# Hybrid DeltaNet and RWKV decoder block on one core: modulation weights bound to steps of the matmul stream, pinned joins, earlier transposes and another prologue

## The chip, the cores and the metric

The kernel runs on one core of one Trainium2 chip. The metric is the device time of one execution in microseconds (us); lower is better. The five engines are named as in the profile: PE (TensorE, matrix products), DVE (VectorE), ACT (ScalarE), POOL (GpSimd) and SP (SyncE, which here only issues DMAs). Each engine works through its own list of instructions in order.

## The reference

One decoder block over 512 tokens of width 1024, in float32. A conditioning vector gives six modulation vectors of 1024; two mixers run beside each other and are merged by gates; a gated feed-forward block with a short convolution follows.

```python
cond = jax.nn.silu(c)
mod = cond @ w_ada[i] + b_ada[i]
shift1, scale1, gate1, shift2, scale2, gate2 = jnp.split(mod[:, None, :], 6, axis=-1)
h = rms_norm(x, norm1_w[i]) * (1.0 + scale1) + shift1
p = h @ w_in[i]
qkv_a, z_a, b_a, a_a, p_b, gl_a, gl_b = split_cols(p, IN_SIZES)
y_a = gated_deltanet(...)      # chunks of 64 tokens, a triangular solve in each
y_b = rwkv7_time_mix(...)      # likewise, computed in chunks by the kernel
merged = sigmoid(gl_a) * (y_a @ w_branch_gdn[i]) + sigmoid(gl_b) * (y_b @ w_branch_rwkv[i])
x = x + gate1 * (merged @ w_out[i])
h = rms_norm(x, norm2_w[i]) * (1.0 + scale2) + shift2
x = x + gate2 * conv_glu(h, w_ffn_in[i], conv_ffn[i], w_ffn_out[i])
return rms_norm(x, norm_f_w)
```

## The kernel before

Activations lie with the features on the 128 partitions and the 512 tokens along the row. A product tile is 128 output features by 512 tokens in one PSUM bank, summed over blocks of 128 input features. Each block takes three matmuls (`mm3`): weights and activations are split into a high part in a shorter format and the float32 remainder, and high·high, high·low and low·high are added. A weight tile arrives as `raw` by DMA, ACT casts it to `whi`, DVE subtracts to `wlo` (`split`).

**The stages**, with their times in the profiled execution: a prologue with the sum of squares of x and the first norm (to 20 us); seven product tiles in which each hidden block is used as soon as it is normed (`first_tiles`, to 61); then the rest of the input projection, as filling between the parts of the two mixers. Each mixer inverts its chunk matrices (`solve`): 32x32 diagonal blocks on DVE and POOL, then the joins, 256 matmuls of 32x32 in two parts with ACT copies between them (L594 and L604, near 205 for the first mixer and 388 for the second), then a recurrence over eight chunks. The products of the first branch (`bg`) start at 335; gate tiles, second branch (`br`), output projection (`o`, residual at L1027) follow, then the second norm (563), the feed-forward products (`fi`, `fo`) and the final norm.

**What sets the order.** Products wait in a list, `queue`. `fill(n)` in the mixers' code draws n groups of three matmuls from it, `need(labels)` draws until given tiles are done, `stream` makes them. A scheduler then moves the emitted instructions by their dependencies and its own model of time; a dependency with the reason "place" binds the order without a semaphore. So what each engine's list looks like is known only after the build.

**The modulation weights.** 48 columns of 128 values, each a dot product of a row of `w_ada` (1024 long, per partition) with the condition. The first 16 (shift and scale of the first norm) are read during the first tiles by `ada`. The other 32 columns are read in halves of 512 (`ada_half`, L208 the DMA, L209 the DVE reduce with its accumulator read), 64 halves in all, with one tile `wada` of one buffer. `product(..., late=n)` asks for n halves when its tile begins; what is left is emitted ahead of `A2`, the scale of the second norm, which needs columns 32 to 39 of `mod`. `mod` 24 to 31 are its shifts; 16 to 23 gate the first residual; 40 to 47 gate the last.

**The second norm.** The residual of the last output tile comes in two halves of 256 tokens (`halves`), so that the norm of the first half (L307 to L309) can begin while PE works on the second.

**Transposes.** `to_natural` turns 128x128 blocks on PE (L616) and copies quarters out of PSUM (L619), for the second mixer after the `bg` products, into another buffer.

Of the kernel before, what the change touches and what calls it, by code (L numbers as in the profile page):

```python
# [23 lines left out]
T = 512  # L24
# [31 lines left out]
def body(ctx, tc, io, out, tap=lambda name, ap: None):  # L56
# [53 lines left out]
    one = const.tile([128, 128], F32, name="one")  # L110
    for k in range(KT):
        sp.dma_start(xT(k), io["xT"][k])
        if k == 3:
            sp.dma_start(cond, io["c"])
    sp.dma_start(cols, io["cols"])
# [12 lines left out]
    kc = const.tile([128, 4], F32, name="kc")  # L128
    for j, v in enumerate((EPS, LNX)):
        pool.memset(kc[:, j:j + 1], v)  # L130
    pool.memset(one, 1.0)
# [46 lines left out]
    last = {"step": None, "hold": False, "gate": None, "norm": None}  # L178
# [4 lines left out]
    def mm3(p, w, j, x, start, stop):  # L183
        hi, lo = (a[j] for a in w)
        xh, xl = x
        i = pe.matmul(p, hi, xh, start=start, stop=False)  # L186
        if last["hold"]:
            tc.add_manual_dep(i.ins, last["step"].ins.name, after, reason="place")
        pe.matmul(p, hi, xl, start=False, stop=False)  # L189
        pe.matmul(p, lo, xh, start=False, stop=stop)  # L190
        return i
# [13 lines left out]
    def ada_half(j, u):  # L205
        w = wp.tile([128, T], F32, name="wada", tag="wada")
        part = slice(T * u, T * u + T)
        sp.dma_start(w, io["w_ada"][j][:, part])  # L208
        i = dve.tensor_tensor_reduce(out=w, in0=w, in1=cond[:, part], scale=1.0,  # L209
                                 scalar=half[:, j:j + 1] if u else col("b_ada", j), op0=ALU.mult, op1=ALU.add,  # L210
                                 accum_out=(mod if u else half)[:, j:j + 1])
        if last["gate"] is not None:
            tc.add_manual_dep(i.ins, last["gate"].ins.name, after, reason="place")
            last["gate"] = None

    first_half = []
# [13 lines left out]
    def stream():  # L230
        while queue:
# [113 lines left out]

    table(SILU)
    fn(cond, cond, AF.Silu)
    table(EXP)
    total = tmp("rs")
    for k in range(KT):  # L350
        sq = total if k == 0 else tmp("sq")
        act.activation(sq, xT(k), AF.Square)
# [3 lines left out]
    pe.matmul(p, one, total, start=True, stop=True)  # L356
# [4 lines left out]
    first_ps = [mm(), mm(), pa(), pa(), pc(), pc(), pc()]  # L361
# [4 lines left out]
    first_w = []  # L366

    def load_ada(k):
        for j in ((0,), (1, 2))[k] if k < 2 else (k + 1,):
            if j < KT:  # L370
                w = slot((2, 3, 8, 9, 12)[j]) if j < 5 else slot2((0, 2, 1)[j - 5])
                first_w.append(w)
                sp.dma_start(w[:, 0:D], io["w_ada"][8 + j])
                sp.dma_start(w[:, D:2 * D], io["w_ada"][j])

    def first_h(k):
# [3 lines left out]
        act.activation(A1[:, k:k + 1], mod[:, 8 + k:9 + k], AF.Identity, scale=col("norm1", k), bias=col("norm1", k))  # L380
# [5 lines left out]
    def inproj(t, evac, psum=mm, begin=None):  # L386
        queue.append(product(t, io["w_in"][t], hx, evac, psum, late=4 if t >= T_GB else 3 if t >= T_GA else 0, begin=begin))
# [99 lines left out]
    last["gate"] = dve.scalar_tensor_tensor(gl, s3, -1.0, bc(nea), op0=ALU.mult, op1=ALU.mult)  # L487
# [65 lines left out]
    def solve(sv, name, work):  # L553
# [9 lines left out]
        sp.dma_start(lt, lsc)  # L563
# [22 lines left out]
        yield  # L586
        for h in range(2):
# [3 lines left out]
            for i in range(16):  # L591
                for e in range(2):
                    lo_r, hi_r = slice(64 * e, 64 * e + 32), slice(64 * e + 32, 64 * e + 64)
                    pe.matmul(p[hi_r, i, :], sv[lo_r, 16 * h + i, 32:64], t1[lo_r, 16 * h + i, :],  # L594
                              start=True, stop=True)
            fill(2)
            for e in range(2):
# [3 lines left out]
            for i in range(16):  # L601
                for e in range(2):
                    lo_r, hi_r = slice(64 * e, 64 * e + 32), slice(64 * e + 32, 64 * e + 64)
                    pe.matmul(p[lo_r, i, :], ht[hi_r, i, :], sv[hi_r, 16 * h + i, 32:64],  # L604
                              start=True, stop=True)
            fill(2)
            for e in range(2):
                lo_r = slice(64 * e, 64 * e + 32)
                act.mul(sv[lo_r, i_, 32:64], p[lo_r], -1.0)

# [98 lines left out]
    for b in range(4):  # L709
# [3 lines left out]
        fill(1)  # L713
    for _ in gsolve:
        pass
# [153 lines left out]
    for ct in range(4):  # L869
        zt, sg = tmp("sg"), tmp("rs")  # L870
        sp.dma_start(zt, zsc[ct])
# [6 lines left out]
    insert([product(("bg", n), io["w_bg"][n], gx, spill(ysc[n])) for n in range(KT)])  # L878
    need(("bg", KT - 1))
# [5 lines left out]
    kb = [ct4(slot(2)), bh]  # L885
    to_natural(bh, lambda e, c: kb[e][hs(e), :, c * C:(c + 1) * C], True)
    to_natural(kh, lambda e, c: kb[e][hs(1 - e), :, c * C:(c + 1) * C], True)
# [124 lines left out]
    for n in range(KT):  # L1012
        if n in (0, 3):
            g = KT - 2 + n // 3
            queue.append(product(T_GB + g, io["w_in"][T_GB + g], hx, last_gate(g), ahead=1))
        queue.append(product(("br", n), io["w_br"][n], bx, merge(n), begin=merge_in(n), ahead=1))
# [88 lines left out]
    for i in range(7, 2 * NF):  # L1105
        queue.append(product(("fi", i), io["w_fi"][i], h2, (glu_up if i % 2 else glu_gate)(i // 2)))
# [38 lines left out]
def _arrays(inputs):  # L1145
# [35 lines left out]
    for e in range(2):  # L1181
# [12 lines left out]
        "c": np.broadcast_to(f["c"], (128, D)),  # L1194
# [29 lines left out]
```

## Time and profile before

| | us |
|---|---|
| median of 3 runs (lowest to highest) | 935.42 (933.39 to 936.28) |
| the profiled execution's own time | 937.31 |
| its span | 935.6 |
| PE busy | 876.3 |
| DVE busy | 533.3 |
| ACT busy | 419.2 |
| mean granted clock of PE | 0.983 |

The span runs from the first to the last instruction; 1.7 us lie around it. A PE that is busy at half the granted clock counts as busy, so a share of 94% is not the share of the full rate. Idle time of PE is told by the instruction that ended it.

### The profile page before, as it was taken

Reading aid. Unit: us, or ns where it says so; the run is one execution under the profiler, and the core shown is the slowest. Engines: PE = TensorE matmul, PEld = TensorE weight load, DVE = VectorE, ACT = ScalarE, POOL = GpSimd, SP = SyncE. Lnnn points to the kernel's source line nnn. Section 1 sums busy time; section 2 is a strip of 40 time slices with the busy share of each in tenths; the row PEclk is TensorE's granted clock in tenths of the full one; section 3 lists DMA queues with packets and bytes.
Section 4 is the critical chain, followed back from the end, with each engine's and each line's share of the span. In section 5 each row is a group of like instructions: output and inputs, shape, how many; then the busy total and the mean of one; then the engine's idle time right before and its main releaser. Section 6 shows DMA issues by size and latency. Waiting matters only on the chain.

```text
span 935.6 us, 13853 instructions
## 1 busy us (share of the span) xinstructions
PE 876.3 (94%) x5459; PEld 687.7 (74%) x5459; DVE 533.3 (57%) x858; ACT 419.2 (45%) x680; POOL 95.2 (10%) x91
## 2 busy tenths in 40 slices
PE   2999999999989978899999999999999999999996
PEld 1886577677656666677668888888888888888885
DVE  5987859824696786255476537564445445332233
ACT  5367543734554747632465335343333333333231
POOL 1000300000352300001230120000000000010112
PEclk9999999997999989899999999999999999999998
DMA  9841245363323367644546542322322322533322
GB/s 332 283 149 67 91 105 185 109 166 112 103 82 113 69 213 267 162 147 148 183 158 202 171 141 84 111 91 92 109 92 90 105 99 90 179 98 100 107 80 91
DMA packets 81119, 125.72 MB, mean 134 GB/s; under 512 B 26045, under 2 KB 42813, under 8 KB 80990
## 3 DMA queue, kind: packets, MB, share of 16 engines
q1 hardware_dynamic: 81054, 124.83, 42.2%
q8 instruction: 43, 0.70, 0.3%
q14 instruction: 22, 0.18, 0.1%
HBM read 110.13 MB, written 14.16 MB: 133 GB/s over the span
## 4 chain that ended last, share of the span: by engine, by line
PE 69%; DVE 10%; DMA 6%; ACT 6%; issue 6%; POOL 2%; SPq 0%; DVEq 0%; POOLq 0%; ACTq 0%
PE ps_mm L186 19%; PE ps_mm L189 18%; PE ps_mm L190 18%; DMA wada<-in_w_ada 4%; DVE wlo L148 2%; PE ps_pc L181 2%; DVE wada L209 1%; ACT tmp_rs L94 1%; PE ps_pc L186 1%; PE ps_pc L189 1%; PE ps_pc L190 1%; ACT slot L619 1%; PE ps_pa L186 1%; PE ps_pa L189 1%; PE ps_pa L190 1%
## 5 line engine op out<-in xcount | busy, mean ns | idle before, releaser
L186 PE MATMUL ps_mm<-hh,whi 128*128 128x512 f32 (+1 forms) x642 | 264.2, 412 | 9.8 <-ACT hh L308 3.4
L148 DVE TENSOR_TENSOR wlo<-raw,whi 128x1024 fp32r<-128x1024 f32 (+2 forms) x140 | 161.2, 1152 | 176.2 <-ACT whi L145 170.6
L190 PE MATMUL ps_mm<-hh,wlo 128*128 128x512 f32 (+1 forms) x642 | 255.0, 399 | 1.3 <-DVE wlo L148 1.3
L189 PE MATMUL ps_mm<-hl,whi 128*128 128x512 f32 (+1 forms) x642 | 253.8, 396 | 0.0
L145 ACT CAST whi<-raw 128x1024 fp32r<-128x1024 f32 (+2 forms) x140 | 137.1, 979 | 259.7 <-PE ps_mm L189 198.4
L186 PEld LDWEIGHTS ps_mm<-hh,whi 128*128 128x128 f32 x642 | 121.5, 190 | 46.8 <-issue 8.5
L190 PEld LDWEIGHTS ps_mm<-hh,wlo 128*128 128x128 f32 x642 | 121.6, 189 | 31.6 <-issue 3.4
L189 PEld LDWEIGHTS ps_mm<-hl,whi 128*128 128x128 f32 x642 | 122.1, 190 | 26.7 <-issue 4.0
L186 PE MATMUL ps_mm<-slot,whi 128*128 128x512 f32 (+1 forms) x226 | 85.7, 379 | 4.7 <-ACT tmp_sp L94 4.7
L190 PE MATMUL ps_mm<-slot,wlo 128*128 128x512 f32 (+1 forms) x226 | 85.1, 376 | 0.0
L189 PE MATMUL ps_mm<-slotd,whi 128*128 128x512 f32 (+1 forms) x168 | 62.4, 371 | 0.0
L186 PEld LDWEIGHTS ps_mm<-slot,whi 128*128 128x128 f32 x226 | 43.2, 191 | 12.6 <-ACT tmp_sp L94 4.9
L190 PEld LDWEIGHTS ps_mm<-slot,wlo 128*128 128x128 f32 x226 | 43.1, 191 | 7.7
L189 PE MATMUL ps_mm<-slot,whi 128*128 128x512 f32 (+1 forms) x122 | 45.3, 372 | 0.0
L186 PE MATMUL ps_mm<-slotd,whi 128*128 128x512 f32 (+1 forms) x96 | 36.4, 379 | 0.0
L190 PE MATMUL ps_mm<-slotd,wlo 128*128 128x512 f32 (+1 forms) x96 | 36.1, 376 | 0.0
L209 DVE CUSTOM_DVE_ANT_0 wada<-wada,cond,cols 128x512 f32<-128x512 f32 x32 | 25.6, 800 | 18.3 <-DMA wada<-in_w_ada 18.2
L189 PEld LDWEIGHTS ps_mm<-slotd,whi 128*128 128x128 f32 x168 | 31.6, 188 | 5.7
L1099 DVE TENSOR_TENSOR tmp_sg<-tmp_acc,ps_mm 128x512 f32<-128x512 f32 x20 | 13.8, 688 | 36.0 <-PE ps_mm L190 35.8
L209 DVE CUSTOM_DVE_ANT_0 wada<-wada,cond,half 128x512 f32<-128x512 f32 x32 | 24.9, 779 | 14.6 <-DMA wada<-in_w_ada 14.4
L398 DVE SCALAR_TENSOR_TENSOR tmp_acc<-ps_mm,cols,tmp_acc 128x511 f32<-128x511 f32 (+2 forms) x44 | 32.8, 746 | 0.7
L1032 POOL COPY tmp_rs<-tmp_sq 128x512 f32<-128x512 f32 x2 | 2.1, 1064 | 304.0 <-ACT tmp_sq L1029 304.0
(270 smaller groups left out, 1262.5 us busy)
## 6 DMA issues: line engine op xcount, KB each, us to landing
raw<-in_w_in SPq DMA_DIRECT2D x40, 512.0 KB, 4.1
raw<-in_w_fi SPq DMA_DIRECT2D x37, 512.0 KB, 3.5
wada<-in_w_ada SPq DMA_DIRECT2D x64, 256.0 KB, 2.7
raw<-in_w_fo SPq DMA_DIRECT2D x16, 512.0 KB, 3.6
slot<-in_w_ada SPq DMA_DIRECT2D x10, 512.0 KB, 8.5
slot<-in_xT SPq DMA_DIRECT2D x16, 256.0 KB, 4.6
raw<-in_w_out SPq DMA_DIRECT2D x8, 512.0 KB, 3.4
raw<-in_w_in SPq DMA_DIRECT2D x8, 448.0 KB, 4.5
```

The costliest lines, as they stand in the source:

```text
L94: i = act.activation(*a, **k)
L145: i = act.copy(hi, src)
L148: j = eng.tensor_tensor(lo, src, hi.bitcast(F32), op=ALU.subtract)
L181: last["step"] = pe.matmul(*a, **k)
L186: i = pe.matmul(p, hi, xh, start=start, stop=False)
L189: pe.matmul(p, hi, xl, start=False, stop=False)
L190: pe.matmul(p, lo, xh, start=False, stop=stop)
L209: i = dve.tensor_tensor_reduce(out=w, in0=w, in1=cond[:, part], scale=1.0, scalar=half[:, j:j + 1] if u else col("b_ada", j), op0=ALU.mult ...
L398: dve.scalar_tensor_tensor(acc[:, i:], p[:, :T - i], w[:, taps - 1 - i:taps - i], acc[:, i:], op0=ALU.mult, op1=ALU.add)
L619: (act.copy if e == c or quiet else dve.tensor_copy)(place(e, 2 * b + c), p[hs(c), :, e, :])
L1032: pool.tensor_copy(sums[0], sq)
L1099: dve.tensor_tensor(t, accs[j], p, op=ALU.mult)
```

## The change

- **Modulation halves at steps.** `ada_half` is parted into a load and a reduce. `stream` spreads an item's halves over its steps: a load ahead of one step, its reduce four steps later, each bound by `at_step` to stand behind the last `mm3` emitted. The counts change: one half with each `RK` and `RR` tile of the second mixer, two with each second gate tile, one with each `br`, three or two with each `o` but the last, one with each `fi`. The loop that emitted the rest ahead of `A2` is gone; the last 16 halves go with `fi`.
- **Pinned joins.** Each join is bound behind the last `mm3` of the filling before it, and the next `mm3` behind the join.
- **Transposes in place.** `to_natural_2` transposes `bh` and `kh` ahead of waiting for `bg`, into the same two buffers; ahead of the second solve's joins stand six groups of filling.
- **Prologue.** The condition comes as one row of 1024 in two pieces, is spread over the partitions by matmuls with a row of ones, and goes through SiLU out of PSUM. The first `w_ada` columns are loaded ahead of the last two blocks of x. Dummy matmuls on a tile of ones (`work`) stand around these.

```diff
-            for _ in range(min(it["late"], len(ada_rest))):
-                ada_half(*ada_rest.pop(0))
+            todo, loaded = min(it["late"], len(ada_rest)), None
+            gap = it["n"] // todo if todo else 0
...
+                    if todo and at % gap == 0 and at // gap < todo:
+                        loaded = ada_load(*ada_rest.pop(0))
                     mm3(p, q["w"], k, it["xs"][at], at == 0, at == it["n"] - 1)
+                    if loaded and at % gap == min(gap - 1, 4):
+                        ada_half(*loaded)
+                        loaded = None
...
+    def at_step(i):
+        if last["mm"] is not None:
+            tc.add_manual_dep(i.ins, last["mm"].ins.name, after, reason="place")
...
+    def work(n, i):
+        for _ in range(n):
+            j = pe.matmul(first_ps[6][:, 0:128], one, one, start=True, stop=True)
...
+    i = work(8, None)
+    for u in range(2):
+        m = pe.matmul(first_ps[u], one[0:1], crow[u], start=True, stop=True)
...
+    i = work(16, i)
...
+    work(10, m)
...
+        def join(*a):
+            last["join"] = pe.matmul(*a, start=True, stop=True)
+            tc.add_manual_dep(last["join"].ins, behind[0].ins.name, after, reason="place")
...
+    need(T_RK + 2)
     for _ in gsolve:
         pass
...
+    to_natural_2(bh, kh)
+    kb = [kh, bh]
     need(("bg", KT - 1))
...
-    to_natural(bh, lambda e, c: kb[e][hs(e), :, c * C:(c + 1) * C], True)
-    to_natural(kh, lambda e, c: kb[e][hs(1 - e), :, c * C:(c + 1) * C], True)
+    fill(6)
     for _ in rsolve:
         pass
...
-        queue.append(product(("o", n), io["w_out"][n], mx, residual(n, x2, 16, keep, total2), late=2, halves=n == KT - 1))
+        queue.append(product(("o", n), io["w_out"][n], mx, residual(n, x2, 16, keep, total2),
+                             late=3 if n < 2 else 2 if n < KT - 1 else 0, halves=n == KT - 1))
     need(("o", KT - 2))
     table(EXP)
-    while ada_rest:
-        ada_half(*ada_rest.pop(0))
     dve.scalar_tensor_tensor(A2, mod[:, 32:40], 1.0, col("norm2", 0, 8), op0=ALU.add, op1=ALU.mult)
```

What stands in the engines' lists at the places that the prediction speaks of. First DVE at the end of the output projection, before; L1027 is the residual out of PSUM, L307 and L309 the norm, `wlo` the weights' remainder:

```order
L1027 SCALAR_TENSOR_TENSOR slot_4387<-ps_mm,mod,slot_4387 128x512
L148 TENSOR_TENSOR wlo<-raw,whi 128x896
L1027 SCALAR_TENSOR_TENSOR slot_4387<-ps_mm,mod,slot_4387 128x256
L307 SCALAR_TENSOR_TENSOR tmp_acc<-slot_4386,A_103,tmp_rs 128x256
L309 SCALAR_TENSOR_TENSOR hl_5079<-tmp_acc,mod,hh_5071 128x256
L1027 SCALAR_TENSOR_TENSOR slot_4387<-ps_mm,mod,slot_4387 128x256
L148 TENSOR_TENSOR wlo<-raw,whi 128x896
L307 SCALAR_TENSOR_TENSOR tmp_acc<-slot_4386,A_103,tmp_rs 128x256 x2
```

The same place after the change, from the last residual (now L1094) on; L223 is the reduce of a half and the read of its accumulator, `A_108` the scale A2, L322 the norm:

```order
L1094 SCALAR_TENSOR_TENSOR slot_4342<-ps_mm,mod,slot_4342 128x256
L223 ISA wada,half<-wada,cond,cols 128x512
L223 ISA half 128x1
...
L223 ISA wada,half<-wada,cond,cols 128x512
L223 ISA half 128x1
L223 ISA wada,mod<-wada,cond,half 128x512
L223 ISA mod 128x1
L1123 SCALAR_TENSOR_TENSOR A_108<-mod,cols 128x8
L322 SCALAR_TENSOR_TENSOR tmp_acc<-slot_4341,A_108,tmp_rs 128x256 x2
```

Between the last residual and `A_108` there are now eight reduces of halves, of which the first and the last two are shown; before, there is none. The norm of the first half of the tokens stood ahead of the last residual and now stands behind it and behind the eight.

SP at this place, after the change: L219 loads a half, L1113 stores a residual tile, L334 loads `fi` weights:

```order
L1113 DMA xsc<-slot_4342 128x256
L219 DMA wada<-in_w_ada 128x512
L334 DMA raw<-in_w_fi 128x7x128
L219 DMA wada<-in_w_ada 128x512 x6
L334 DMA raw<-in_w_fi 128x7x128 x4
```

Six loads of halves now stand in a row ahead of four loads of `fi` weights; before, there are no loads of halves at this place.

PE at the joins of the first solve, before; L594 and L604 are the two kinds of joins, L181 and L726 belong to the recurrence:

```order
L594 MATMUL ps_pa<-slot_957,slotd_851 32x32 x31
L604 MATMUL ps_pa<-slotd_851,tmp_sg 32x32
L594 MATMUL ps_pa<-slot_957,slotd_851 32x32 x32
L604 MATMUL ps_pa<-slotd_851,tmp_sg 32x32 x63
L181 MATMUL ps_pc<-slot_1319,slotd_851 64x64 x8
```

The same after the change, where both kinds have one line, L633, and L191, L196 and L197 are the three matmuls of a group:

```order
L633 MATMUL ps_pa<-slot_997,slotd_891 32x32 x32
L191 MATMUL ps_mm<-hh_109,whi 128x512
L196 MATMUL ps_mm<-hl_117,whi 128x512
L197 MATMUL ps_mm<-hh_109,wlo 128x512
L191 MATMUL ps_mm<-hh_110,whi 128x512
L196 MATMUL ps_mm<-hl_118,whi 128x512
L197 MATMUL ps_mm<-hh_110,wlo 128x512
L633 MATMUL ps_pa<-slotd_891,tmp_sg 32x32 x32
```

Two groups of three now stand between one set of 32 joins and the next, where the sets followed one another.

More of the change, by code (lines that the diff above doesn't have):

```diff
@@ L175, in block_sum @@
         pe.matmul(p, ones_r, lo, start=False, stop=True)
-    last = {"step": None, "hold": False, "gate": None, "norm": None}
+    last = {"join": None, "mm": None, "step": None, "hold": False, "norm": None}
     def step(*a, **k):
@@ L186, in mm3 @@
         i = pe.matmul(p, hi, xh, start=start, stop=False)
+        if last["join"] is not None:
+            tc.add_manual_dep(i.ins, last["join"].ins.name, after, reason="place")
         if last["hold"]:
@@ L189, in mm3 @@
         pe.matmul(p, hi, xl, start=False, stop=False)
-        pe.matmul(p, lo, xh, start=False, stop=stop)
+        last["mm"] = pe.matmul(p, lo, xh, start=False, stop=stop)
         return i
@@ L203, in ada, with ada_load, ada_half @@
             tc.add_manual_dep(i.ins, last["norm"].ins.name, after, reason="place")
-    def ada_half(j, u):
+    def at_step(i):
+        if last["mm"] is not None:
+            tc.add_manual_dep(i.ins, last["mm"].ins.name, after, reason="place")
+    def ada_load(j, u):
         w = wp.tile([128, T], F32, name="wada", tag="wada")
[L207 to L216, printed above, removed]
+        at_step(sp.dma_start(w, io["w_ada"][j][:, T * u:T * u + T]))
+        return j, u, w
+    def ada_half(j, u, w):
+        at_step(dve.tensor_tensor_reduce(out=w, in0=w, in1=cond[:, T * u:T * u + T], scale=1.0,
+                                         scalar=half[:, j:j + 1] if u else col("b_ada", j), op0=ALU.mult, op1=ALU.add,
+                                         accum_out=(mod if u else half)[:, j:j + 1]))
     ada_rest = [(j, u) for j in range(16, 48) for u in range(2)]
@@ L355, in body @@
     p = pa()
-    pe.matmul(p, one, total, start=True, stop=True)
+    m = pe.matmul(p, one, total, start=True, stop=True)
+    tc.add_manual_dep(m.ins, i.ins.name, after, reason="place")
+    work(10, m)
     rstd = tmp("rs")
     whole = [rstd_of(p, 1.0 / D, rstd)]
-    first_ps = [mm(), mm(), pa(), pa(), pc(), pc(), pc()]
     hx = list(zip(hh, hl))
     made = []
-    first_w = []
     def load_ada(k):
@@ L609, in solve, with to_natural_2 @@
                 act.mul(sv[lo_r, i_, 32:64], p[lo_r], -1.0)
+    def to_natural_2(x, y):
+        for b in range(4):
+            ps_ = [pa().rearrange("p (h e k) -> p h e k", h=4, e=2) for _ in range(2)]
+            for p, src in zip(ps_, (x, y)):
+                for ct in range(4):
+                    pe.transpose(p[:, ct].rearrange("p e k -> p (e k)"), src[:, ct, 128 * b:128 * b + 128], ident)
+            for c in range(2):
+                for e in range(2):
+                    for p, o in zip(ps_, (hs(e), hs(1 - e))):
+                        at = slice(128 * b + 64 * c, 128 * b + 64 * c + 64)
+                        act.copy((x if e else y)[o, :, at], p[hs(c), :, e, :])
+            fill(1)
     def to_natural(src, place, quiet=False):
@@ L870, in body @@
         zt, sg = tmp("sg"), tmp("rs")
-        sp.dma_start(zt, zsc[ct])
+        i = sp.dma_start(zt, zsc[ct])
+        tc.add_manual_dep(i.ins, last["load"].ins.name, after, reason="place")
         fn(zt, zt, AF.Silu)
@@ L1105, in body @@
     for i in range(7, 2 * NF):
-        queue.append(product(("fi", i), io["w_fi"][i], h2, (glu_up if i % 2 else glu_gate)(i // 2)))
+        queue.append(product(("fi", i), io["w_fi"][i], h2, (glu_up if i % 2 else glu_gate)(i // 2), late=1))
     prefetch()
```

69 lines of the change are left out of this document (47 added, 22 removed).

## The prediction

> **What bounds the kernel now.** I read the page first, then the idle time of TensorE (PE) by what ended it, then the granted clock in stretches, and last the timeline at the places that the change touches. The page says that PE is the engine to watch: the other three are far from full.
>
> ```profile
> PE 876.3 (94%) x5459; PEld 687.7 (74%) x5459; DVE 533.3 (57%) x858; ACT 419.2 (45%) x680; POOL 95.2 (10%) x91
> PEclk9999999997999989899999999999999999999998
> ```
>
> So time can be won in two ways only: PE idles less, or it is granted the full clock for longer. The second row shows four places before the middle where a slice loses clock. The list of PE's waits gives the first kind (total us, times, longest):
>
> ```profile
> PE ps_pa L356 <- DVE tmp_rs L354: 15.4, 1, 15.4
> PE ps_mm L186 <- ACT tmp_sp L94: 4.7, 1, 4.7
> PE ps_pa L616 <- ACT slot L619: 2.9, 6, 1.3
> PE ps_pa L604 <- ACT tmp_sg L599: 2.7, 4, 0.7
> PE ps_pa L760 <- DVE tmp_sq L756: 1.9, 3, 0.7
> PE ps_pc L181 <- DVE ck L793: 1.6, 2, 1.3
> PE ps_mm L186 <- DVE slot L398: 1.5, 1, 1.5
> PE ps_mm L190 <- DVE wlo L148: 1.3, 2, 0.8
> PE ps_pc L181 <- DVE cz L785: 1.2, 2, 0.7
> PE ps_pa L635 <- DVE slotd L639: 1.1, 1, 1.1
> PE ps_pa L518 <- DVE tmp_acc L514: 1.1, 1, 1.1
> ```
>
> The second kind shows in a table by stretch. Its columns are busy time (and instructions) of PE, its weight loads, DVE, ACT and POOL; then the granted clock, the DMA share and GB/s:
>
> ```profile
> 206.00:210.00 4.00, 2.66 (x156) 2.44 (x150) 0.75 (x1) 2.72 (x5) 0.00 (x0) 1.00 0.00 0
> 210.00:214.00 4.00, 4.00 (x115) 3.55 (x108) 0.64 (x2) 3.33 (x5) 0.00 (x0) 0.55 0.03 8
> 214.00:218.00 4.00, 4.00 (x18) 1.90 (x17) 3.19 (x5) 2.44 (x5) 0.00 (x0) 0.50 0.49 149
> 218.00:222.00 4.00, 4.00 (x14) 3.15 (x13) 0.76 (x2) 0.00 (x0) 0.00 (x0) 0.67 0.73 220
> 334.00:338.00 4.00, 3.27 (x8) 2.59 (x9) 3.93 (x10) 1.68 (x4) 0.81 (x1) 0.50 0.38 144
> 338.00:342.00 4.00, 4.00 (x15) 3.15 (x14) 3.76 (x13) 1.11 (x2) 0.00 (x0) 0.73 0.37 129
> 389.00:392.00 3.00, 1.79 (x89) 1.56 (x83) 0.00 (x0) 1.16 (x2) 0.00 (x0) 0.89 0.99 338
> 392.00:396.00 4.00, 4.00 (x97) 3.72 (x92) 0.20 (x1) 2.73 (x5) 0.00 (x0) 0.50 0.49 186
> 396.00:400.00 4.00, 4.00 (x41) 2.86 (x41) 1.42 (x4) 1.81 (x3) 0.00 (x0) 0.73 0.02 4
> ```
>
> A busy PE at clock 0.50 does half the work. After the first row (the first solve's joins, still at full clock) the next three (the end of the joins and the recurrence's start) lose 4 × (0.45 + 0.50 + 0.33) = 5.1 us, the two after the 4.7 us wait 3.27 × 0.50 + 4 × 0.27 = 2.7, the last three (second joins) 3 × 0.11 + 4 × (0.50 + 0.27) = 3.4.
>
> All sums below are made against the profiled execution, 937.3 us (span 935.6 and 1.7 around it). It lies 1.9 above the median of the runs shown, 935.4, so 1.9 is taken off at the end.
>
> **The change part by part**
>
> *The weight halves at the second norm.* This term decides, so it comes first. Each half is one DMA into the only `wada` buffer, one DVE reduce out of it, and only then the next DMA. The trace has this round:
>
> ```profile
> 231.16 0.75 DVE L209 CUSTOM_DVE_ANT_0 wada<-wada,cond,cols 128x512 f32<-128x512 f32 x1 [3.58 <-DMA wada<-in_w_ada]
> 231.83 0.08 DVE L209 DVE_READ_ACCUMULATOR2_ANT half<- 128x1 f32 x1
> 231.94 0.33 SPq L208 DMA_DIRECT2D wada<-in_w_ada  x1
> 234.57 0.75 DVE L209 CUSTOM_DVE_ANT_0 wada<-wada,cond,half 128x512 f32<-128x512 f32 x1 [0.44 <-DMA wada<-in_w_ada]
> ```
>
> One round takes 234.57 − 231.16 = 3.41 us: 0.75 for the reduce, then 2.6 from the issue on SP to the next reduce. Before, the order has none of them near the second norm. After, it has, on DVE, eight halves in a row between the last residual of the output projection and `A_108`, the scale that the second norm multiplies by, and SP has their loads in one block of six ahead of the `fi` weights. DVE works in order, and every norm of the second hidden tile is behind those eight. Here is the place in the trace of before:
>
> ```profile
> 561.27 0.48 DVE L307 SCALAR_TENSOR_TENSOR tmp_acc<-slot,A,tmp_rs 128x256 f32<-128x256 f32 x1 [2.57 <-ACT tmp_rs L94]
> 562.50 0.47 PE L186 MATMUL ps_mm<-hh,whi 128*128 128x256 f32 x1
> 562.74 0.48 DVE L1027 SCALAR_TENSOR_TENSOR slot<-ps_mm,mod,slot 128x256 f32<-128x256 f32 x1
> ```
>
> Today the first half of the tokens is normed (561.27) before the last residual (562.74), and PE goes from the projection to the next product with no gap. After the change DVE finishes that residual at 563.2, does the first half (its load is in), and begins the eighth 7 × 3.41 = 23.9 later, at 587.1. That one ends at 587.9, `A_108` at about 588.1, and PE starts 1.23 later (from 561.27 to 562.50 above), at 589.3: 26.8 us after 562.50, with nothing else in PE's list. Then it restarts cold, 2.7 by the rows at 334 to 342. Against that stand the small pauses that PE now makes there while it runs beside the residual, about 1.5 (an estimate). I take **+28** (25 to 30: a round of 3.3, or one load that lands late).
> The Trainium skill, "TensorE: Matmul & The Clock Gate", Part 1: The HAM clock gate, has the full clock return after about 3.4 us of sustained work. By that the restart would cost half of 3.4, 1.7 us, and the sum would be 1 lower; the rows above show over 5 us at half clock, and I go by them.
>
> *The other pinned halves.* Some leave the stretch from 90 to 190, where PE waits for DVE at L518, L635, L398 and L148: 1.1 + 1.1 + 1.5 + 1.3 = 5.0. Not all of it is their doing (a product's own subtraction stands there too): a third, **−1.7** (0 to −4). Sixteen or so leave the first recurrence, where PE waits for L756, L793 and L785: 1.9 + 1.6 + 1.2 = 4.7. About half, **−2.5** (−1 to −5). Forty now go with the gate, branch and output products. What they have as cover is matmul time, and its unit is the spacing of two matmuls:
>
> ```profile
> 203.93 0.39 PE L190 MATMUL ps_mm<-hh,wlo 128*128 128x512 f32 x1
> 204.16 0.39 PE L186 MATMUL ps_mm<-hh,whi 128*128 128x512 f32 x1
> 204.38 0.39 PE L189 MATMUL ps_mm<-hl,whi 128*128 128x512 f32 x1
> ```
>
> An output product is 24 matmuls of 0.226, 5.4 us; the change gives it two or three halves, 6.8 or 10.2 us of rounds. So the halves fall behind there, and the order shows it: some ten between the first and the last residual, eight left over. Where DVE waits for a load ahead of an eviction, PE still has its second bank; I take **+1** (0, if that always covers, to +6, about one wait of 0.6 with each of ten halves). The last sixteen go with the `fi` products, two to three rounds' time for each, and nothing waits for them: 0.
>
> *First joins pinned.* Before, the order has 32 joins, another 32, then the rest with no product between, so PE waits twice for the ACT copy (0.7 each) and then runs at half clock. After, two 3-matmul groups stand behind each 32: 6 × 0.226 = 1.36 us of work over a pair of copies of 1.18 (L599, below).
>
> ```profile
> 206.84 1.18 ACT L599 COPY tmp_sg<-ps_pa 32x512 f32<-32x512 f32 x2 [0.43 <-PE ps_pa L594]
> ```
>
> If both the wait (1.35) and the clock (5.1) come back, 6.5; I take **−5.5** (−3 to −7), since the loose products were filling something before.
>
> *Second joins pinned.* The same edit, with the same pattern in the order: 1.35 of waits and 3.4 of clock; **−4** (−2 to −5).
>
> *Transposes in place and sooner.* Thirty-two transposes and 32 ACT copies move from behind the `bg` products to ahead of them. The transposes and the copies of before, and where `bg` starts now:
>
> ```profile
> L616 PE MATMUL ps_pa<-cons,slot 128*128 128x128 f32 x64 | 9.8, 280 | 3.2 <-ACT slot L619 2.6 <-ACT slotd L619 0.6
> L619 ACT COPY slot<-ps_pa 64x256 f32<-64x256 f32 x72 | 26.5, 368 | 9.7 <-PE ps_pa L616 8.7
> 334.74 0.79 PE L186 MATMUL ps_mm<-slot,whi 128*128 128x512 f32 x1 [4.70 <-ACT tmp_sp L94]
> ```
>
> The 28 copies that stand ahead of the gate's SiLU on ACT take 28 × 0.37 = 10.3 us, so `bg` starts over 10 us later than 334.74. The 32 transposes themselves (half of 9.8, 4.9) and four 3-matmul groups between them (4 × 0.68 = 2.7) fill part of it, and 10.3 − 7.6 = 2.7 is left; with the pauses between the pieces I make it +4. The waits for these copies later (L619, 2.9) go, −3. The rsolve's 1024-wide copy now stands on ACT among the `bg` evictions and can hold them for about 3 (an estimate: its width is near that of eight copies of 256, 8 × 0.37). Sum **+4** (0 to +8).
>
> *Prologue.* The condition as one row saves a 0.5 MB load, and dummy matmuls keep PE at work before the first product.
>
> ```profile
> 15.36 2.04 PE L356 MATMUL ps_pa<-tmp_rs,one 128*128 128x512 f32 x2 [15.36 <-DVE tmp_rs L354]
> 20.38 1.22 PE L186 MATMUL ps_mm<-hh,whi 128*128 128x512 f32 x2 [2.98 <-ACT hh L308]
> 26.34 0.40 PE L189 MATMUL ps_pc<-hl,whi 128*128 128x512 f32 x1
> 313.62 1.13 PE L861 MATMUL ps_pa<-tmp_sq,ones_r 128*128 128x512 f32 x2 [0.49 <-ACT slotd L849]
> ```
>
> The total's matmul takes 2.04 cold and about 1.1 warm (a like form, L861): −0.9 on the chain to the norm. From 20.38 to 26.34 fourteen matmuls take 5.96 against 14 × 0.226 = 3.16: 2.8 lost to the clock, though DVE's norm chain hides some. The loads of xT and the squares still set when the total is ready, about 15 us. I take **−2.3** (−0.5 to −3.5).
>
> *The rest, at 0.* The products that are asked for ahead of the first joins are work that comes anyway. The z loads of the first branch's gate stand on SP behind the second solve's `lt` load, one issue of 0.33 as in the row of SP above; the first scale on DVE instead of ACT is one instruction on one column.
>
> Sum: +28 − 1.7 − 2.5 + 1 − 5.5 − 4 + 4 − 2.3 = **+17.0**. 937.3 + 17.0 = 954.3, and 952.4 against the median.
>
> **The rivals**
>
> *The clock is not won back (17%).* The joins are 32x32 matmuls; it may be they that let the clock fall, not the two waits, and six full matmuls between them may not hold it. Then only the waits go, 1.35 + 1.35, instead of 9.5: the result is 6.8 higher, 959.2. For it: the clock is still 1.00 in the row up to 210, with both waits in it, and falls while PE is busy. Against: it falls right after a stretch that idled for a third. The Trainium skill, "TensorE: Matmul & The Clock Gate", section Why this matters for your kernels, asks for no idle gaps of over about 3 us between bursts; by that, waits of 0.7 would cost no clock, and this rival would hold.
>
> *The stall is not there (5%): faster.* If the eight loads did not go round one by one, because each had landed before DVE came to it, the eight halves would cost 8 × 0.83 and mostly lie beside PE's last products. Then the rest alone counts: the terms but +28 sum to −11.0, and 937.3 − 11.0 − 1.9 = 924.4. It decides where eight rounds take under 11 us, 1.4 each. Against: one buffer, and the row above with 2.6 from issue to reduce.
>
> *The pinned work was worth far more than I took (8%).* The clock lost is 11.2 in the three stretches and 2.8 in the prologue, and the waits after the prologue in the list above sum to 20.0: 34 in all. To outweigh +28 the change must win five sixths of that; with all of it, 937.3 − 34 + 28 − 1.9 = 929.4. This needs waits with other causes (the 4.7 at 334.74) to go too. I give 4% to that and 4% to a time within the bound.
>
> **How the numbers follow.** My forecast has 70%, and its own range is 952 ± 8: the bounds above, not all at the same end. The rival on the clock lies at 959 with like bounds. The range 943 to 962 holds these two but for their outer tails, about 8 in 10. About 0.3% (2.8 us) is what a measurement of this kernel can tell from no change: faster by more 9%, within 4%, slower by more 87%.
>
> **What would show it.** In the profile after: PE idle for 25 us or more near 555 to 585, ended by ACT's `hh`, behind DVE's reduces of `wada`, which wait for DMA seven times by 2.6 us; clock 0.50 for some 5 us after it. At the joins: no wait of 0.7 on the copy, and a clock of 1.00 for the following 10 us (the rival: still 0.50). Less than 15 us of idle at the second norm would make the prediction wrong, and so would halves that DVE reads before the last residual.

## The result and the profile after

| | before | after |
|---|---|---|
| median of four runs, us | 935.85 (933.39 to 938.29) | 972.90 (968.77 to 974.81) |
| span of the profiled execution | 935.6 | 973.1 |
| PE busy | 876.3 | 889.0 |
| mean granted clock | 0.983 | 0.975 |

The ratio of after to before is 1.0397, 95% interval 1.0377 to 1.0416: slower by 37 us, where 17 were forecast and 943 to 962 was the range.

The list of PE's waits after the change (total us, times, longest), the first rows and two others, answers to the list of before:

```profile
PE ps_mm L191 <- ACT hh L323: 26.9, 2, 26.1
PE ps_mm L197 <- DVE wlo L153: 7.5, 9, 1.6
PE ps_mm L191 <- ACT whi L150: 6.2, 4, 1.7
PE ps_mm L191 <- ACT tmp_sp L94: 5.6, 1, 5.6
PE ps_pa L1105 <- ACT tmp_sq L1096: 3.8, 3, 2.3
...
PE ps_pa L633 <- ACT tmp_sg L648: 0.6, 1, 0.6
```

One wait of 26.1 us on the second norm's `hh` is new. The wait for the copies between the joins, 2.7 in four, is 0.6 in one. New beside it is 7.5 us in nine waits for the remainder of a weight tile, `wlo`, where before had 1.3 in two.

The timeline of DVE at the second norm shows the stall; the bracket is the idle time before an instruction and what ended it:

```profile
570.38 0.48 DVE L1094 SCALAR_TENSOR_TENSOR slot<-ps_mm,mod,slot 128x256 f32<-128x256 f32 x1 [2.63 <-PE ps_mm L197]
570.79 0.74 DVE L223 CUSTOM_DVE_ANT_0 wada<-wada,cond,cols 128x512 f32<-128x512 f32 x1
...
574.31 0.75 DVE L223 CUSTOM_DVE_ANT_0 wada<-wada,cond,half 128x512 f32<-128x512 f32 x1 [1.77 <-DMA wada<-in_w_ada]
...
578.27 0.75 DVE L223 CUSTOM_DVE_ANT_0 wada<-wada,cond,cols 128x512 f32<-128x512 f32 x1 [3.20 <-DMA wada<-in_w_ada]
...
596.27 0.75 DVE L223 CUSTOM_DVE_ANT_0 wada<-wada,cond,half 128x512 f32<-128x512 f32 x1 [2.96 <-DMA wada<-in_w_ada]
...
597.06 0.17 DVE L1123 SCALAR_TENSOR_TENSOR A<-mod,cols 128x8 f32<-128x8 f32 x1
```

The eight halves stand between the last residual and the scale. From the first to the eighth it takes 596.27 − 570.79 = 25.5 us, seven rounds of 3.64. PE's timeline shows when the next product starts:

```profile
598.35 0.80 PE L191 MATMUL ps_mm<-hh,whi 128*128 128x256 f32 x2 [26.07 <-ACT hh L323]
```

The chain that ended last, followed back in time, runs through the same rounds and shows how one is made up (start, us, what; the two pieces of 0.03 and 0.09 between a landing and its reduce are left out):

```profile
582.77 2.56 DMA wada<-in_w_ada
585.46 0.75 DVE wada L223
586.25 2.60 DMA wada<-in_w_ada
588.98 0.75 DVE wada L223
589.77 2.65 DMA wada<-in_w_ada
```

**Where the 37 us arose.** To place the rest, I count the product matmuls (those of the groups of three; a 128x512 as one, a 128x256 as a half) from the start of each trace, and read the time at which the same count has ended. Differences to before:

| matmuls done, and the stage | after minus before | change in the stage | forecast |
|---|---|---|---|
| 200, first tiles | −3.6 | −3.6 | −2.3 |
| 500, to the first solve | −6.2 | −2.6 | −1.7 |
| 650, first solve's joins and the recurrence's start | −6.0 | +0.2 | −5.5 |
| 1000, recurrence, first branch, transposes, second joins | −8.3 | −2.2 | −2.5 |
| 1200, second recurrence | −6.5 | +1.8 | 0 |
| 1500, second branch and output products | +3.0 | +9.5 | +1 |
| 1600, second norm | +36.5 | +33.6 | +28 |
| 3050, near the end | +37.1 | +0.6 | 0 |

Up to the second recurrence the changed kernel is ahead; it loses it all and more in the last three stages before the feed-forward products. The clock at the joins did come back, as these rows show; their columns are those of the table by stretch in the prediction:

```profile
190.00:200.00 10.00, 7.78 (x36) 5.68 (x38) 5.21 (x9) 2.51 (x4) 0.00 (x0) 0.83 0.51 156
200.00:210.00 10.00, 10.00 (x278) 8.08 (x271) 2.55 (x4) 5.53 (x10) 0.00 (x0) 1.00 0.34 110
210.00:220.00 10.00, 10.00 (x46) 8.28 (x45) 5.11 (x8) 3.82 (x5) 0.00 (x0) 1.00 0.32 91
```

The joins (199.8 to 209.2) lie almost wholly in the second row, at full clock and with no idle time; the loss of clock and 2.2 us of idle time stand in the row ahead of them.

### The profile page after: what moved, and what is told of

Same layout as the page of the kernel before. It is cut to its first block, busy times and chain, and to the rows that moved or that the text cites. A ratio compares the mean times of both kernels' runs of the same rounds, so it can differ in the third digit from the quotient of the medians.

```text
span 973.1 us, 13995 instructions
## 1 busy us (share of the span) xinstructions
PE 889.0 (91%) x5531; PEld 694.7 (71%) x5531; DVE 535.4 (55%) x859; ACT 417.6 (43%) x680; POOL 92.6 (10%) x91
## 4 chain that ended last, share of the span: by engine, by line
PE 62%; DMA 12%; DVE 10%; ACT 9%; issue 5%; POOL 1%; SPq 0%; DVEq 0%; ACTq 0%; POOLq 0%
PE ps_mm L191 17%; PE ps_mm L197 16%; PE ps_mm L196 16%; DMA wada<-in_w_ada 8%; PE ps_pc L186 3%; DVE wlo L153 2%; DMA raw<-in_w_in 2%; DVE wada L223 1%; ACT tmp_rs L94 1%; ACT whi L150 1%; PE ps_pc L191 1%; PE ps_pc L196 1%; PE ps_pc L197 1%; PE ps_pa L633 1%; ACT slot L673 1%
## 5 line engine op out<-in xcount | busy, mean ns | idle before, releaser
L191 PE MATMUL ps_mm<-hh,whi 128*128 128x512 f32 (+1 forms) x642 | 260.5, 408 | 37.0 <-ACT hh L323 26.9
L197 PE MATMUL ps_mm<-hh,wlo 128*128 128x512 f32 (+1 forms) x642 | 253.2, 396 | 2.8 <-DVE wlo L153 2.8
L196 PE MATMUL ps_mm<-hl,whi 128*128 128x512 f32 (+1 forms) x642 | 253.4, 396 | 0.0
L191 PEld LDWEIGHTS ps_mm<-hh,whi 128*128 128x128 f32 x642 | 121.0, 189 | 72.7 <-ACT hh L323 28.0
L197 PEld LDWEIGHTS ps_mm<-hh,wlo 128*128 128x128 f32 x642 | 121.1, 189 | 32.5 <-DVE wlo L153 5.0
L196 PEld LDWEIGHTS ps_mm<-hl,whi 128*128 128x128 f32 x642 | 121.4, 189 | 26.5 <-issue 4.0
L191 PE MATMUL ps_mm<-slot,whi 128*128 128x512 f32 (+1 forms) x226 | 86.3, 383 | 6.1 <-ACT tmp_sp L94 5.6
L197 PE MATMUL ps_mm<-slot,wlo 128*128 128x512 f32 (+1 forms) x226 | 85.8, 380 | 4.7 <-DVE wlo L153 4.7
L196 PE MATMUL ps_mm<-slotd,whi 128*128 128x512 f32 (+1 forms) x168 | 62.7, 374 | 0.0
L191 PEld LDWEIGHTS ps_mm<-slot,whi 128*128 128x128 f32 x226 | 43.6, 193 | 14.7 <-ACT tmp_sp L94 6.0
L197 PEld LDWEIGHTS ps_mm<-slot,wlo 128*128 128x128 f32 x226 | 43.4, 192 | 14.6 <-DVE wlo L153 7.2
L196 PE MATMUL ps_mm<-slot,whi 128*128 128x512 f32 (+1 forms) x122 | 45.4, 372 | 0.0
L223 DVE CUSTOM_DVE_ANT_0 wada<-wada,cond,half 128x512 f32<-128x512 f32 x32 | 26.0, 814 | 27.3 <-DMA wada<-in_w_ada 27.0
L223 DVE CUSTOM_DVE_ANT_0 wada<-wada,cond,cols 128x512 f32<-128x512 f32 x32 | 25.4, 793 | 25.7 <-DMA wada<-in_w_ada 25.6
L191 PE MATMUL ps_mm<-slotd,whi 128*128 128x512 f32 (+1 forms) x96 | 36.4, 379 | 0.0
L196 PEld LDWEIGHTS ps_mm<-slotd,whi 128*128 128x128 f32 x168 | 32.1, 191 | 5.9 <-DVE slotd L153 0.2
L197 PE MATMUL ps_mm<-slotd,wlo 128*128 128x512 f32 (+1 forms) x96 | 36.1, 376 | 0.0
L94 ACT ACTIVATE tmp_acc<-tmp_acc 128x512 f32<-128x512 f32 x22 | 13.9, 633 | 41.6 <-DVE tmp_acc L441 41.5
```

Source lines behind the costliest of these rows:

```text
L94: i = act.activation(*a, **k)
L197: last["mm"] = pe.matmul(p, lo, xh, start=False, stop=stop)
L223: at_step(dve.tensor_tensor_reduce(out=w, in0=w, in1=cond[:, T * u:T * u + T], scale=1.0, scalar=half[:, j:j + 1] if u else col("b_ada", j ...
```

## The experiments

Theory at the outset: the halves' rounds through one buffer make the loss, at the second norm and from the gate to the output products; the other parts win what they won before 1000 matmuls. Rivals: another part takes part in the loss; a round costs PE the same wherever it stands; not the buffer but the transfers or DVE's order set the pace. All times are medians, and each run of before was on the same chip.

### The halves alone

```diff
 # in outline: the kernel before, with from the change only
+    ada_load / ada_half with at_step, the new counts, the loop ahead of A2 removed
```

> The kernel before with nothing but the pinned modulation halves (loads and reduces at steps, with the new counts). Theory (the one-buffer rounds cost all of the loss and more): by the time at equal work in the two traces, the second norm costs +33.5 and the gate, branch and output products +10.6, less some 2 to 3 gained before 200 us: 976 (968 to 984), slower than the whole change or as slow, with PE idle for over 25 us ahead of the second norm. Rival (the halves alone cost the stall that was predicted, 28, and the other 10 come from the pinned joins or the transposes): 961 to 966.

974.4 us, ratio 1.0416 (1.0387 to 1.0445). PE's longest wait is the same one:

```profile
PE ps_mm L186 <- ACT hh L315: 28.8, 2, 25.8
```

So the pinned halves alone make the kernel as slow as the whole change. At equal work (the same count of product matmuls) this run is 5.6 ahead of before at 1200 matmuls, loses 6.9 to 1500 and 33.1 to 1600. The rival, a stall of 28 and nothing else, is too low.

### The change with the halves of before

```diff
-            todo, loaded = min(it["late"], len(ada_rest)), None
+            for _ in range(min(it["late"], len(ada_rest))):
+                ada_half(*ada_rest.pop(0))
...
+    while ada_rest:
+        ada_half(*ada_rest.pop(0))
```

> The whole change but with the halves as before (asked for at the start of an item, old counts, the rest ahead of the second norm's scale). Theory: no stall at the second norm and no lag in the gate to output products, so what is left of the change shows: the prologue's 3.2, and 2 to 3 from the second joins with the transposes; 928 (921 to 933). Rival (joins, transposes or prologue cost something themselves): 936 or more.

937.5, ratio 1.0032 (1.0015 to 1.0049): the loss is gone, as the theory has it, but what is left of the change wins nothing, and the value forecast for it fell. At equal work it is 11.0 ahead at 650, with 4.9 of that won at the first joins, and 1.7 ahead at 1000. Two places take the lead away. Between 750 and 850 matmuls, where the transposes and their copies now stand ahead of the first branch's products, 12.1 are lost. Behind that, PE's timeline shows a wait:

```profile
372.03 0.28 PE L624 MATMUL ps_pa<-slot,slotd 32*32 32x32 f32 x2 [2.18 <-DMA slot<-tsc_r]
376.09 1.91 PE L624 MATMUL ps_pa<-slot,slotd 32*32 32x32 f32 x62 [3.77 <-DMA slot<-tsc_r]
```

PE reaches the second solve's joins before the solve's scratch loads have landed, and since the joins are pinned there it waits.

### Two halves at the second mixer's first tiles

```diff
-        ..., late=2 if t >= T_GB else 1 if T_RK <= t < T_RV else 0,
+        ..., late=2 if t >= T_GB else 2 if T_RK <= t < T_RV else 0,
```

> The change with two halves instead of one at each of the eight first tiles of the second mixer, so that eight fewer are left behind; in the order of DVE one half stands ahead of the scale and none between the scale and the norm. Theory: the stall of 33 goes but for some 2; eight more rounds in the recurrence cost 0 to 5 there; the gate to output products keep most of their 10: 942 (934 to 950). Rival (a round costs PE its 3.4 us wherever it stands, so the eight are only moved): 960 to 968.

944.2, ratio 1.0101 (1.0080 to 1.0122), as the theory said. Eight rounds begun earlier take 28.7 us out of the kernel. So the rival is refuted: what a round costs PE depends on where it stands. At equal work 8.0 are still lost between 1200 and 1500: the later products ask for as many halves as before, now for columns that nothing waits for.

### A second buffer

```diff
+        last["turn"] = not last["turn"]
+        if last["turn"] and j >= 20:
+            w = tp.tile([128, 1024], F32, name="pr", tag="pr")[:, 0:T]
+        else:
+            w = wp.tile([128, T], F32, name="wada", tag="wada")
```

> The change with every other half behind the recurrences loaded into the solves' scratch tile, so that two buffers alternate and the next load is under way while DVE waits. In the order no half is left between the last residual and the second norm but one. Theory (one buffer sets the round of 3.4 to 3.7): stall gone, and the gate to output products lose 2 to 5 instead of 10: 934 (927 to 942). Rival (DVE's order or the transfer itself sets the pace, not the buffer): over 955.

936.6, ratio 1.0011 (1.0001 to 1.0022). The stall is gone (0.9 from 1500 to 1600): with two loads on their way, the halves are through before the last residual. Yet 7.5 are lost from 1200 to 1500, where I had expected 2 to 5 and the change loses 9.5. Most of that part does not hang on the single buffer.

### The joins alone, and with the prologue

```diff
 # in outline: the kernel before, with from the change only
+    join(), last["join"], need(T_RK + 2), fill(6)         (joins alone)
+    crow, work(8), work(16), work(10), the new loads      (with the prologue)
```

> The kernel before with the pinned joins alone (six groups of filling ahead of the second solve's joins with them). Theory (both solves lose their waits and their half clock, 5 at each by the run with the old halves, first solve, and by the whole change, second): 926 (922 to 930). Rival (the clock or a later stage takes it back, as in the run with the old halves, whose second solve waited 6 us for its scratch loads): 933 or more.

> The kernel before with prologue and pinned joins, old halves, old transposes. Theory: the prologue's 3.2 at equal work stays to the end, so 3 below the run with the joins alone: 923 (919 to 928). Rival (a gain made ahead of the first solve is lost at the next wait that does not depend on PE): level with the joins alone.

Joins alone 927.1, ratio 0.9903 (0.9879 to 0.9927); with the prologue 927.3, ratio 0.9898 (0.9869 to 0.9928). Both are faster than before and than the change. The clock holds through the joins and after them:

```profile
200.00:210.00 10.00, 10.00 (x220) 7.99 (x219) 2.66 (x5) 6.11 (x9) 0.00 (x0) 1.00 0.27 95
210.00:220.00 10.00, 10.00 (x59) 8.06 (x57) 5.19 (x8) 2.48 (x4) 0.00 (x0) 1.00 0.55 177
```

Between 500 and 650 matmuls the joins alone win 5.2, between 750 and 1050 another 7.0. With the prologue the kernel is 3.5 further ahead at 500 matmuls, 0.3 at 750, and no longer ahead at the end. Where the lead goes shows in the wait at the first solve's joins, first with the joins alone, then with the prologue:

```profile
197.57 1.19 PE L592 MATMUL ps_pa<-slot,slotd 32*32 32x32 f32 x62 [0.60 <-DMA slot<-tsc_g]
```

```profile
195.79 1.26 PE L622 MATMUL ps_pa<-slot,slotd 32*32 32x32 f32 x62 [2.36 <-DMA slot<-tsc_g]
```

The lead of PE turns into a longer wait for the solve's loads; the rival held.

### One product more ahead of the first joins

```diff
-    need(T_RK + 2)
+    need(T_RK + 3)
```

> Prologue and pinned joins, with one product more asked for ahead of the first solve's joins (5.4 us of matmuls). Theory (the prologue's gain is lost in the wait of 2.4 for the solve's scratch load, which does not depend on PE's pace): with more cover that wait goes and 2 come back: 925 (923 to 927.5). Rival (the gain is lost later, at the 4.2 us wait ahead of the first branch's products): 927 as before, with the wait gone.

926.8, ratio 0.9901 (0.9878 to 0.9925). The wait of 2.36 is gone, but nothing is won by it: the profile has 1.71 us for a weight tile at 201 in its place, and the kernel is level with the one without the added product, 0.9 behind it in the traces. The rival is nearer, with the loss earlier than it said.

### The transposes alone

```diff
+    to_natural_2(bh, kh)
+    kb = [kh, bh]
     need(("bg", KT - 1))
...
+    fill(6)
```

> The kernel before with the transposes in place and sooner alone (and the six groups of filling). Theory (28 copies of 0.37 on ACT ahead of the gate, given back only in part by the pauses that go later): 939 (935 to 943). Rival (they start the second solve sooner and win 3 or more): 932 or less.

936.1, ratio 1.0002 (0.9987 to 1.0017): no difference, so neither the theory nor the rival. My price of 4 was not there.

### The pinned halves without the new transposes

> Prologue, pinned joins and the pinned halves with the second buffer, with the transposes as before. Theory: against the run of the whole change with the second buffer (936.6) the transposes' 3 to 4 go: 933 (927 to 938), above the run with the old halves by what the pinned halves still cost from the gate to the output products. Rival (the pinned halves win in the recurrences what the old ones lose): below the run with prologue and joins.

934.4, ratio 0.9985 (0.9970 to 0.9999). Against the run with the second buffer and the transposes (936.6) it is 2.2 lower, 4.2 in the traces. So with the joins pinned the earlier transposes do cost something, and alone they don't. The halves of before show it more strongly: the run with the old halves (937.5) and that with prologue and joins (927.3) differ in nothing but the place and buffer of the transposes and the order of the z loads, and lie 10 apart. At equal work 7.5 are lost from 1200 to 1500 here.

### Small matmuls between the joins

```diff
-            fill(2)
+            d = pa()
+            for i in range(64):
+                behind[0] = pe.matmul(d[0:32, 0:32], one[0:32, 0:32], one[0:32, 0:32], start=True, stop=True)
...
```

> The kernel before with the pinned joins, but with 64 matmuls of 32x32 between the sets instead of two groups of products. These are extra work, read from a tile of ones and used by nothing. Theory (PE's waits of 0.7 let the clock fall): PE has no waits there, the clock stays near 1.00 and the time is within 5 of the run with the joins alone, 927 to 933. Rival (the small matmuls themselves count too little and products between them hold the clock): clock 0.5 for some 10 us behind the joins, 935 to 945.

981.3 (two runs), ratio 1.0486 (1.0446 to 1.0526). The 64 matmuls took 4.3 us the first time and 6.7 at half clock, instead of the 1.4 of two groups, so the time says little; the clock decides:

```profile
200.00:210.00 10.00, 10.00 (x276) 9.22 (x275) 3.79 (x5) 3.83 (x5) 0.00 (x0) 0.88 0.17 60
210.00:220.00 10.00, 10.00 (x230) 10.00 (x229) 1.69 (x5) 2.33 (x4) 0.00 (x0) 0.50 0.47 157
220.00:230.00 10.00, 10.00 (x231) 10.00 (x230) 1.76 (x5) 1.18 (x2) 0.00 (x0) 0.50 0.19 56
```

PE is busy all the time, with no wait, and falls to half clock: the unbroken row of 32x32 matmuls begins at 203.0, and the clock is 0.50 from 207.6 to 238.3. So waits of 0.7 are not needed for the clock to fall, and my theory is refuted. A stretch of 32x32 matmuls does it by itself; with full products between the joins it held (1.00 in both rows of the joins alone).

### The remainder on POOL

```diff
-        split(hi[:, :n], lo[:, :n], raw[:, :n])
+        split(hi[:, :n], lo[:, :n], raw[:, :n], pool if last["pool"] else dve)
```

> The whole change, but from the second branch's products to the output projection the weights' remainder is subtracted on POOL instead of DVE, so that it no longer stands behind the reduces that wait for their loads. In the order of DVE seven halves instead of eight are left ahead of the norm. Theory (the 10.6 that the whole change loses from the gate to the output products is PE waiting for the remainder, L153, behind those reduces): some 7 of it and one round, 3.6, go: 962 (957 to 967). Rival (the raw weights themselves come late, since their DMAs stand on SP behind loads of halves that wait for the buffer; or POOL is too slow and takes the place): 969 or more.

979.3, ratio 1.0471 (1.0440 to 1.0501), a miss. Between 480 and 560 us PE waits for `wlo` only once more (0.25 us). It waits instead for the evictions on DVE behind the same reduces, and later for POOL's sum of squares:

```profile
492.26 0.77 PE L191 MATMUL ps_mm<-hh,whi 128*128 128x512 f32 x1 [2.92 <-DVE tmp_acc L1059]
556.48 0.59 PE L191 MATMUL ps_mm<-slot,whi 128*128 128x512 f32 x1 [3.90 <-DVE slot L1095]
571.82 1.22 PE L1105 MATMUL ps_pa<-tmp_rs,one 128*128 128x256 f32 x2 [5.17 <-POOL tmp_rs L1102]
```

The remainder was only what PE met first behind a DVE that waits. POOL took 2.4 us for a remainder of 1024 columns, DVE 1.25.

### Fewer halves there, and their loads on another queue

With two halves at the first tiles of the second mixer and two buffers, first with the counts of the change elsewhere, then with none at the second branch, then (on the kernel of 934.4) with the loads issued from POOL:

```diff
-        ..., merge(n), late=1, begin=merge_in(n), ...
+        ..., merge(n), begin=merge_in(n), ...
...
-        at_step(sp.dma_start(w, ...
+        at_step((pool if j >= 20 else sp).dma_start(w, ...
```

> Prologue, pinned joins, pinned halves with the second buffer, and two halves instead of one at the first tiles of the second mixer, so that the gate to output products carry fewer. Theory: of the 6 that the pinned halves lost there against the old ones with two buffers, over half comes back: 930 (926 to 934). Rival (the reduces' place on DVE, not the number of halves left, costs there, or the first solve loses what the output stage gains): 934 or more.

> Prologue, pinned joins, two buffers, two halves at the first tiles of the second mixer, and none with the second branch's products: in the order of DVE 2 halves are left among the merges instead of 13. Theory (reduces that wait for their loads among the merges cost the 7): against the run with two at the first tiles (939.5) the loss between the recurrences and the output products goes from 7 to 2 or less: 933 (929 to 936). Rival (loads on SP, or the halves cost the same wherever they stand): 937 or more.

> Prologue, pinned joins and two buffers (934.4), but the loads of the halves behind the recurrences are issued from POOL's queue instead of SP's. Rival theory (loads that wait for a free buffer hold up the branch's own loads behind them on SP): the loss of 7 shrinks to 3 or less, 930 (927 to 932). Theory (reduces on DVE): no gain, 933 to 938.

The first took 939.5, ratio 1.0036 (1.0010 to 1.0062), the second 936.4 (1.0022, 1.0002 to 1.0042), the third 950.5 (1.0155, 1.0139 to 1.0171). The first came out as its rival said: at equal work it loses 7.7 from 1200 to 1500, no less than with eight halves fewer read ahead of this stretch (7.5). Without halves at the branch that loss is 1.2 (prologue and joins, with the halves of before: 0). PE's waits between 470 and 525 us, with the counts of the change and two buffers (934.4):

```profile
PE ps_mm L197 <- DVE wlo L153: 3.4, 4, 1.1
PE ps_mm L191 <- ACT slot L150: 1.0, 1, 1.0
PE ps_mm L191 <- DVE tmp_acc L1045: 0.5, 1, 0.5
```

With none at the branch the same question has an empty answer: no wait is left there. The median fell by only 3, within what these runs scatter (931.4 to 941.9), and 3.6 were lost at the second norm instead, so the time is above what the theory gave. The trace is that of the shortest of the ten runs, so the 1.2 may be on the low side. Issuing the loads from POOL made it worse than either side had it: 17.4 are lost from 1200 to 1500, DVE still waits for the loads, and POOL's own sums stand behind issues that wait for a buffer (PE waits 4.1 us for one). So this run does not decide whether SP's queue takes part.

## Why the prediction was wrong

The mechanism that was to decide did decide, at its place, and the change is slower as forecast; but two terms of the sum were mis-sized, which makes 14 of the 20 us that are missing, and a gain of 5.5 did not come.

- **The stall at the second norm: +28 forecast, +33.6 measured.** Right in kind: eight halves, one buffer, PE idle for 26.1, then 0.50 to 0.58 of the clock to about 604. The long wait itself was sized well: 26.1 against 26.8, though a round took 3.64 and not 3.41. What was too small lies ahead of it. I let the last output product end undisturbed, but DVE met a waiting reduce ahead of the first half of the last residual as well:

```profile
563.34 0.75 DVE L223 CUSTOM_DVE_ANT_0 wada<-wada,cond,cols 128x512 f32<-128x512 f32 x1 [3.17 <-DMA wada<-in_w_ada]
...
565.02 0.48 DVE L1094 SCALAR_TENSOR_TENSOR slot<-ps_mm,mod,slot 128x256 f32<-128x256 f32 x1
```

PE's list has the sums of squares (L1104 and L1105) in the middle of that product, and they waited, the first two for residuals behind such reduces:

```profile
562.35 0.70 PE L1104 MATMUL ps_pa<-tmp_rs,one 128*128 128x256 f32 x2 [1.20 <-POOL tmp_rs L1101]
566.06 1.22 PE L1105 MATMUL ps_pa<-tmp_sq,one 128*128 128x256 f32 x2 [2.30 <-ACT tmp_sq L1096]
571.58 0.70 PE L1105 MATMUL ps_pa<-tmp_sq,one 128*128 128x256 f32 x2 [0.80 <-ACT tmp_sq L1096]
```

That makes 4.3, where the same stretch of before has 0.7 in two waits; I had taken off 1.5 for these, an estimate that no row gave. And the clock fell once more, ahead of the stall:

```profile
566.00:569.00 3.00, 2.94 (x11) 2.76 (x12) 0.76 (x2) 0.90 (x3) 0.00 (x0) 0.50 0.79 228
```

With this, some 4 us of clock are lost in the stage, not 2.7. The stall was undone by starting eight rounds earlier and by a second buffer, so its cause is shown and not only argued.

- **The forty halves with gate, branch and output products: +1 forecast, +9.5 measured.** This step failed. The prediction said that "PE still has its second bank", which covers a late eviction. It left out what else stands on DVE behind a waiting reduce: the remainder of the next weight tile and the merges. PE's waits in the changed kernel between 485 and 561 us, where the kernel before has none in its like stretch:

```profile
PE ps_mm L197 <- DVE wlo L153: 5.0, 5, 1.6
PE ps_mm L191 <- DVE tmp_acc L1059: 1.6, 2, 1.2
```

In all seven, the DVE instruction waited for stands behind a reduce; the rest of the 9.5 is mostly in the matmuls right behind each wait, which follow one another more slowly. One place:

```profile
516.40 0.75 DVE L223 CUSTOM_DVE_ANT_0 wada<-wada,cond,cols 128x512 f32<-128x512 f32 x1 [0.93 <-DMA wada<-in_w_ada]
517.08 0.08 DVE L223 DVE_READ_ACCUMULATOR2_ANT half<- 128x1 f32 x1
517.08 1.22 DVE L153 TENSOR_TENSOR wlo<-raw,whi 128x1024 fp32r<-128x1024 f32 x1
```

```profile
518.36 0.50 PE L197 MATMUL ps_mm<-slot,wlo 128*128 128x512 f32 x1 [1.60 <-DVE wlo L153]
```

It also looked at output products, which are 24 matmuls long; the loss is at the branch products, 12 matmuls or 2.7 us with one round of 3.4 each. With none there the loss fell from 7.7 to 1.2. A second buffer took DVE's waits for these loads between 478 and 526 us from 7.9 to 5.0, but the loss only from 9.5 to 7.5. How much of it is waiting and how much the reduces' own time on DVE stays open. So does the part of the loads themselves: without halves at the branch their transfers and their places in SP's queue are gone as well, and no run parts these from the reduces.

- **The first joins: −5.5 forecast, +0.2 measured.** The edit brings 4.9 and 5.2 in two runs with the halves of before, and 2.0 in that with the prologue, where the wait for the scratch loads takes the rest. In the whole change it is used up ahead of the joins, where four waits for a weight tile stand between 177 and 193, 1.47 + 0.53 + 1.71 + 0.93 = 4.6, and the clock drops to 0.83. Of these only one, 0.74, is there in the run with the old halves; the first two are there with the halves alone as well (1.49 and 0.52). The prediction priced the halves that leave this stretch and gave no price to those that come to the second mixer's first tiles. By which route these bring the waits is not shown: the weights' casts are late on ACT, and no reduce that waits for its load stands in front of them. The last two also come with the old halves and one product more (1.71 and 0.53).

- **The rival on the clock** fell: it came back, 1.00 in the rows after the joins. The Trainium skill, "TensorE: Matmul & The Clock Gate", section Why this matters for your kernels, names idle gaps; the trace of the run with small matmuls between the joins shows the clock at 0.50 with no gap at all. That rival's suspicion of the small matmuls was right, but its fear that products between them would not hold the clock was not borne out.

- **The second joins and the transposes** (−4 and +4): the sum for the stage, −2.2 with the recurrence, was right. The parts were not: the joins alone bring 7.0 there, and the transposes alone cost nothing. Beside pinned joins the transposes cost 4 in the traces with pinned halves and two buffers, the price that was forecast, but 10 with the halves of before. The forecast that the first branch's products would start some 10 us late held: the change was 8.5 ahead at 750 matmuls, and yet they start at 336.24 instead of 334.74. Most of this came back behind them. Why more comes back in some of these kernels than in others stays open.

- **The prologue** (−2.3) gained 3.6, 6.2 with what follows it, but beside the pinned joins alone none of it reaches the end. The prediction added gains at the front to the end time without asking what comes next that does not depend on PE: the first solve's scratch loads or, with one product more ahead of them, a weight tile.

- **The bound on what could be won**, 34, was too low by some 6: the list of waits that it sums leaves out rows of before with 2.1 (L398), 1.7 (L145), 1.2 (L408) and 1.1 us (L861). The forecast does not rest on it.

## What to carry to other kernels

A transfer that goes round one buffer has a rate of its own; before pinning such transfers to steps of a faster stream, add up the rounds and the time of the steps, and see in the order what is left at the next consumer. A reduce that may wait for its load holds everything behind it on its engine, evictions and weight preparation alike, so the second PSUM bank is not its cover. Time won ahead of a wait that does not depend on the busy engine can be lost there again: of the three gains, only that of the pinned joins, 9 us, reached the end, and the version with the joins alone (927.1) beats both kernels.

## What was not expected of the hardware

Matmuls of 32x32 back to back, with PE busy in every slice, fell to a granted clock of 0.50 after 4.6 us and kept it for over 20 us; six 128x512 matmuls after every 32 joins kept it at 1.00. The 256 KB loads in the stall took 2.56 to 3.04 us by the chain, so that the same round varied between 3.5 and 4.0; in the longest, a `fi` weight load had been issued 2.5 us earlier.
